# Where a two-layer diffusion and expert kernel loads its branch registers, makes its first weight splits and stores its output

## The chip, the cores and the metric

The kernel runs on one core of a Trainium2 chip. The metric is the device time of one execution in microseconds. Three runs of the kernel before gave 1623.38, 1624.77 and 1629.05 us; their median, 1624.77 us, is the time to compare with.

## The reference, cut to what matters

Two layers run over 256 latent tokens (and 256 context tokens) of width 1024. The change touches only the end of the second layer, a mixture of eight experts:

```python
logits = xt @ router_w + router_b            # 256 tokens, 8 experts
top_val, top_idx = lax.top_k(logits, 2)      # each token goes to its two best experts
gates = jax.nn.softmax(top_val)
# for each expert e, on the tokens that chose it:
y_e = (silu(x_e @ w1[e]) * (x_e @ w3[e])) @ w2[e]     # w1, w3: 1024x3584, w2: 3584x1024
out[token] += gate * y_e[token]
# behind it
xl = xl + g2 * out
return rms_norm(xl, final_g)
```

Everything is float32. An expert has 42 MB of weights and all eight are read once, 336 MB in all.

## The kernel before

**Places.** The experts are worked on one after the other in an order chosen at run time by how many tokens each has; the position in that order is called a place (0 to 7). Each place is cut into seven slices of 512 hidden columns. A slice is three steps on TensorE: `up` (the products with w1 and w3), `flip` (four or two transposes that turn the gated result so that it can be a stationary operand) and `lower` (the product with w2). `body(g)` runs `up` of slice g, then `lower` of slice g-1, then `flip` of slice g.

**Two ways to multiply.** Places 0, 1, 3, 5 and 7 are "raw" (`NAT` and `TWO`): at most 64 tokens, the float32 weights go straight into TensorE (`up_nat` with L1398, `flip_nat` with L1417 and the copy L1419, `down_nat` with L1428). Places 2, 4 and 6 hold up to 128 tokens and are "split" places: ScalarE casts each weight chunk of 128x1024 to a rounded high part (L163), VectorE subtracts it from the raw chunk to get the low part (L164), and TensorE makes three fast products with the parts (`mm3`, L266 to L268). The parts live in a ring of four chunks, `W_O` in the tiles R3 to R6. While a raw place runs, these tiles are lent out as extra landing room for weights (`lend`) and then taken back (`take_back`).

**Order of the work.** From the experts on, the program is written in manual order: what is called first stands first in each engine's queue, and each engine works through its queue in order. `w_split(n)` writes casts and subtractions until n chunks are split; `w_next` calls it so that the splits stay three chunks ahead of the products. An `agenda` of small steps (gathers of the next place, scatters of the last one) is run down between the products. `w_dma` puts the next 1 MB weight tile on SyncE's queue as soon as the written order has released a slot.

**Branches.** Places 0 and 7 exist in two versions, for up to 64 and for up to 128 tokens. `either` loads the count into a register of every engine (`values_load`, L1608), and a `tc.If(n > 64)` (L1610) picks the version. Behind place 7 a third branch, `tc.If(rv > 0)` (L1684, its register from L1683), runs an overflow pass for experts with more tokens than their place holds; with these inputs it is jumped over. The final norm (`inv_rms`, L735 and L256 to L262), the scaling (L1716, L1717) and the two stores (L1719) stand behind it.

**The end of place 7.** `scat_now` takes the expert's sum out of PSUM: weighted by the gate (first L1437), cast to a high part, the low part subtracted, eight products with the one-hot matrix (L1445, L1446), four additions to the tokens (L1450). `ends` then squares and sums each half row on ScalarE (L1643) and multiplies it by the final gain on GpSimd (L1644).

Of the kernel before, what the change touches and what calls it, by code (L numbers as in the profile page):

```python
# [8 lines left out]
F32 = mybir.dt.float32  # L9
# [6 lines left out]
P = 128  # L16
# [18 lines left out]
def tile_hybrid_headgroup_dit_moe(ctx: ExitStack, tc: tile.TileContext, a, out: bass.AP):  # L35
# [1383 lines left out]
            nc.scalar.copy(hs[n], b[:, 0:256])  # L1419
        return hs  # L1420

    def down_nat(p, i, hs, yas):
        for r in range(2):
            j, raw = raw_tile(("moe_w2", p, i))
            for jj in range(2):
                for hid_, ya in zip(hs, yas):
                    for hf in range(2):
                        nc.tensor.matmul(ya[64 * hf:64 * hf + 64, :], hid_[:, jj * P + 64 * r:jj * P + 64 * r + 64],  # L1428
                                         raw[:, 2 * hf + jj], start=i == 0 and r == 0 and jj == 0,
                                         stop=i == NSL - 1 and r == 1 and jj == 1, skip_group_check=True)  # L1430
                step()
            release(j)

    def scatter_nat(ya, v, g):
# [16 lines left out]
                r += [product, add]  # L1451
        return r

    def up(e, i, h, nxt):
        b1, b3 = bank(), bank()
        for w, b in (("moe_w1", b1), ("moe_w3", b3)):
            for c in range(4):
                wh, wl = nxt((w, e, i))
                for kk in range(2):
                    k = 2 * c + kk  # L1460
                    mm3(b, h.h[:, k], h.l[:, k], wh[:, kk * 512:kk * 512 + 512], wl[:, kk * 512:kk * 512 + 512],
                        k == 0, k == 7)
            if w == "moe_w1":
                s = sbuf[i % 2]
                nc.scalar.activation(s, b1, AF.Silu)
        nc.vector.tensor_mul(s, s, b3)
        return s
# [8 lines left out]
        nc.vector.tensor_sub(hl, b, hh)  # L1476
        return hh, hl

    def down(e, i, hth, ya, nxt):
        hh, hl = hth  # L1480
        for c in range(4):
            wh, wl = nxt(("moe_w2", e, i))
            for jj in range(2):
                j = c // 2 * 2 + jj
                mm3(ya[c % 2], hh[:, j * P:j * P + P], hl[:, j * P:j * P + P], wh[:, jj * 512:jj * 512 + 512],
                    wl[:, jj * 512:jj * 512 + 512], i == 0 and j == 0, i == NSL - 1 and j == 3)
# [54 lines left out]
    SCAT_N = [2, 6, 6, 14, 15, 18, 19, 34, 35, 38, 39]  # L1541
    ya = {}

    def lower(g, nat, two=False):
        e1, i1 = divmod(g, NSL)
        if i1 == 0:
            ya[e1] = [bank("acc") for _ in range(1 + two if nat else 2)]
        if nat:
            down_nat(e1, i1, hts.pop(g), ya[e1])
        else:  # L1550
            down(e1, i1, hts.pop(g), ya[e1], moe_next)
        if i1 == 4:
            gc = list(place(e1))[1]
            sl[:] = [slots(e1, one_hot(e1), gc)] + ([slots(e1, oh_2, gc, 1)] if two else [])
        if i1 == NSL - 1 and 0 < e1 < NE - 2:
            scat(e1, nat)
# [4 lines left out]
    def body(g, nat, two=False):  # L1561
        e, i = divmod(g, NSL)
        s = up_nat(e, i, two) if nat else up(e, i, hg[e], moe_next)
        if g and g - 1 in hts:
            lower(g - 1, nat if i else e - 1 in RAW, two)
            if i == 0 and 1 < e < NE - 1 and nat:
                lend(3, 4, 5, 6)
        hts[g] = flip_nat(g, s, two) if nat else flip(g, s)

    sl = []  # L1570

# [11 lines left out]
    def scat_now(p, more=None):  # L1583
        at = [0, 1, 2, 3, 4, 3, 5, 3, 6, 3, 7]
        for n, (y, (v, g)) in enumerate(zip(ya[p], sl)):
            plan_late(scatter_nat(y, v, g), [8 * n + x for x in at])
        if more is not None:
            plan_late(more, [8 * len(sl) + x for x in (-4, -3, -2, -1)])
        for fs in agenda:
            run(fs)  # L1590
        del agenda[:]
# [12 lines left out]
        scat_now(0)  # L1604


    def either(count, way):
        n = nc.values_load(count[0:1, 0:1], min_val=0, max_val=256)  # L1608
        saved, ends_at = state(), []
        with tc.If(n > 64) as cmp:  # L1610
            way(True)
# [7 lines left out]
            assert len(u) == len(v) and all(c is d or c == d or isinstance(c, tuple) and c[0] == d[0] and c[1] is d[1]  # L1619
                                            for c, d in zip(u, v)), x  # L1620

    either(first_n, first_place)
    take_back(0)
    regs.clear()
    LIM[0] = None
    for g in range(NSL, (NE - 1) * NSL):
        e, i = divmod(g, NSL)
        if i == 0:
            plan_late(fetch(e + 1, e + 1 in RAW), GATH)
        body(g, e in NAT)  # L1630
        if e in NAT and i == NSL - 1:
            take_back(3, 4, 5, 6)
            w_split(st["use"] + NW)
    lower((NE - 1) * NSL - 1, False)
# [10 lines left out]
    def last_place(two):  # L1645
# [4 lines left out]
            body((NE - 1) * NSL + i, True, two)  # L1650
        lower(LAST, True, two)
        nc.gpsimd.dma_start(fg, a["final_g"].to_broadcast([P, D]))
        scat_now(NE - 1, [lambda t=t, hf=hf: ends(t, hf) for hf in range(2) for t in range(2)])

    either(last_n, last_place)
    take_back(3, 4, 5, 6)


# [21 lines left out]
        return nxt  # L1680

    rest_r = [0]
    rv = nc.values_load(cmax[0:1, 0:1], min_val=0, max_val=256)  # L1683
    with tc.If(rv > 0):  # L1684
        for p in range(NE):
            nc.vector.tensor_scalar(posp[:, :, p], posp[:, :, p], 64.0 if p in NAT else 128.0, None, op0=OP.subtract)
# [23 lines left out]
        for t in range(2):  # L1710
            for hf in range(2):
                ends(t, hf)


    r = inv_rms(ss)
    nc.scalar.activation(xg[:, 0], xg[:, 0], AF.Copy, scale=r[:, 0:1])  # L1716
    nc.vector.tensor_scalar(xg[:, 1], xg[:, 1], r[:, 1:2], None, op0=OP.mult)  # L1717
    for t in range(2):
        (nc.scalar, nc.sync)[t].dma_start(out[t * P:t * P + P], xg[:, t])  # L1719


# [75 lines left out]
```

## Time and profile before

| | |
|---|---|
| three runs | 1623.38, 1624.77, 1629.05 us; median 1624.77 |
| the profiled execution | 1627.35 us, of which the span from the first to the last instruction is 1625.6 us |
| TensorE busy | 1561.9 us (96%) |
| VectorE, ScalarE, GpSimd busy | 933.0, 724.9, 25.9 us |
| mean granted TensorE clock | 0.978 |
| read from memory | 489.36 MB, 302 GB/s over the span |

The profiled execution has its own time, and a sum made from its rows is made against that. The trace can be asked for the order of time (what each engine did from when to when, and what ended the idle time before it), for the waits of an engine added up by what ended them, for all instructions of a line of the kernel, and for the busy time in any stretch. The busy share of TensorE says little by itself, since matmuls are pipelined and their ends are modelled; what it waited for is the better question.

### The profile page before, as it was taken

What the parts mean: (1) busy time and instruction counts of PE and PEld (TensorE: products, weight loads), DVE (VectorE), ACT (ScalarE), POOL (GpSimd) and SP (SyncE); (2) the same over time, 40 slices, a digit from 0 to 9 for tenths busy, and PEclk for the clock granted to TensorE, in tenths of its full rate; (3) what the DMA queues carried; (4) which work ended last, traced back from release to release, by engine and by line L of the source; (5) the groups of instructions that cost most, each with busy time, mean ns of one, the idle gap of its engine ahead of it and who ended that gap; (6) DMA issues with size and microseconds to landing.
All of it is one profiled execution on the core that took longest, in us unless ns stands there. A gap on an engine that the chain in (4) does not pass through costs nothing. (4 is left out here: it accounts for less than half of the span.)

```text
span 1625.6 us, 23224 instructions
## 1 busy us (share of the span) xinstructions
PE 1561.9 (96%) x8938; PEld 1161.5 (71%) x8938; DVE 933.0 (57%) x1587; ACT 724.9 (45%) x1085; POOL 25.9 (2%) x54
## 2 busy tenths in 40 slices
PE   7999999999999999999998999999999999999895
PEld 5787788888888887887654557875577855678652
DVE  3794578976564699856201038871188821688411
ACT  4446556222223474565311137761277711677301
POOL 0100000000000001000000000000000000000001
PEclk9999899999999999999799999999999999999998
DMA  8635323756674545547799999999999999999993
GB/s 349 241 137 187 121 83 130 273 200 234 218 276 167 184 165 185 199 181 266 303 421 421 421 421 420 422 403 422 420 421 421 384 420 421 421 421 385 396 420 130
DMA packets 69230, 492.09 MB, mean 303 GB/s; under 512 B 7984, under 2 KB 8752, under 8 KB 9712
## 3 DMA queue, kind: packets, MB, share of 16 engines
q1 hardware_dynamic: 67856, 486.97, 75.3%
q0 software_dynamic: 816, 2.72, 0.6%
q8 instruction: 76, 1.25, 0.3%
q10 hardware_dynamic: 432, 0.74, 0.2%
q14 instruction: 50, 0.41, 0.1%
HBM read 489.36 MB, written 1.05 MB: 302 GB/s over the span
## 5 line engine op out<-in xcount | busy, mean ns | idle before, releaser
L164 DVE TENSOR_TENSOR R<-FA,R 128x1024 fp32r<-128x1024 f32 x366 | 441.7, 1229 | 132.2 <-ACT R L163 128.1
L163 ACT CAST R<-FA 128x1024 fp32r<-128x1024 f32 x366 | 380.2, 1053 | 226.6 <-PE mm L268 142.4
L266 PE MATMUL mm<-R,R 128*128 128x512 f32 (+1 forms) x976 | 369.0, 379 | 9.8 <-ACT R L163 4.4
L267 PE MATMUL mm<-R,R 128*128 128x512 f32 (+1 forms) x976 | 364.1, 373 | 4.2 <-DVE R L164 2.3
L268 PE MATMUL mm<-R,R 128*128 128x512 f32 (+1 forms) x976 | 363.2, 372 | 0.0
L266 PEld LDWEIGHTS mm<-R,R 128*128 128x128 f32 x976 | 184.8, 190 | 48.4 <-ACT R L163 5.1
L266 PE MATMUL acc<-R,R 128*128 128x512 f32 (+1 forms) x552 | 208.2, 378 | 4.9 <-DVE R L788 1.8
L267 PEld LDWEIGHTS mm<-R,R 128*128 128x128 f32 x976 | 185.4, 190 | 36.2 <-DVE R L164 3.2
L268 PEld LDWEIGHTS mm<-R,R 128*128 128x128 f32 x976 | 185.3, 190 | 32.0
L268 PE MATMUL acc<-R,R 128*128 128x512 f32 (+1 forms) x552 | 204.6, 371 | 0.0
L267 PE MATMUL acc<-R,R 128*128 128x512 f32 (+1 forms) x552 | 204.5, 370 | 0.0
L1398 PE MATMUL mm<-FA 128*64 128x256 f32 x1408 | 163.8, 385 | 0.8 <-DVE FA L1450 0.8
L1398 PEld LDWEIGHTS mm<-FA 128*64 128x64 f32 x1408 | 98.8, 138 | 53.8 <-issue 7.4
L266 PEld LDWEIGHTS acc<-R,R 128*128 128x128 f32 x552 | 104.8, 190 | 26.4 <-issue 3.4
L268 PEld LDWEIGHTS acc<-R,R 128*128 128x128 f32 x552 | 104.4, 189 | 17.9 <-issue 0.3
L267 PEld LDWEIGHTS acc<-R,R 128*128 128x128 f32 x552 | 104.7, 190 | 16.5 <-issue 0.3
L1409 DVE TENSOR_TENSOR FA<-FA,mm 128x256 f32<-128x256 f32 x35 | 14.7, 421 | 152.6 <-PE mm L1398 152.6
L1428 PE MATMUL acc<-FA 128*64 128x512 f32 x424 | 99.0, 596 | 1.0 <-ACT FA L1419 1.0
L333 DVE SCALAR_TENSOR_TENSOR FA<-FA 128x1024 f32<-128x1024 f32 x80 | 94.4, 1222 | 5.7 <-DMA FA<-in_w_modt_dram 5.6
L499 DVE SCALAR_TENSOR_TENSOR FA<-FA,pv 128x512 f32<-128x512 f32 (+1 forms) x128 | 74.3, 616 | 1.2 <-ACT FA L495 0.7
L1343 DVE TENSOR_TENSOR R<-lc,R 128x128 fp32r<-128x128 f32 x24 | 7.0, 293 | 118.0 <-ACT R L1340 118.0
L1419 ACT COPY FA<-mm 128x256 f32<-128x256 f32 x35 | 13.1, 373 | 132.3 <-PE mm L1417 132.3
(275 smaller groups left out, 1397.8 us busy)
## 6 DMA issues: line engine op xcount, KB each, us to landing
FA<-in_moe_w_dram SPq DMA_DIRECT2D x264, 1024.0 KB, 15.3
R<-in_moe_w_dram SPq DMA_DIRECT2D x72, 1024.0 KB, 14.4
FA<-in_w_modt_dram SPq DMA_DIRECT2D x28, 1024.0 KB, 4.8
FA<-in_ffn_dram SPq DMA_DIRECT2D x22, 1024.0 KB, 4.8
FA<-in_ffn_w_dram SPq DMA_DIRECT2D x22, 1024.0 KB, 4.8
FA<-in_w_mod_dram SPq DMA_DIRECT2D x20, 1024.0 KB, 6.4
FA<-in_w_in_dram SPq DMA_DIRECT2D x20, 1024.0 KB, 4.8
FA<-in_w_out_dram SPq DMA_DIRECT2D x12, 1024.0 KB, 4.8
```

Source lines behind the costliest of these rows:

```text
L163: nc.scalar.copy(wh, raw)
L164: nc.vector.tensor_sub(wl, raw, wh)
L266: nc.tensor.matmul(ps, ll, rh, start=start, stop=False, skip_group_check=True)
L267: nc.tensor.matmul(ps, lh, rl, start=False, stop=False, skip_group_check=True)
L268: nc.tensor.matmul(ps, lh, rh, start=False, stop=stop, skip_group_check=True)
L333: nc.vector.scalar_tensor_tensor(o, raw[:, c], 1.0, csb[:, s], op0=OP.mult, op1=OP.mult, accum_out=modT[l][:, 2 * r + c, s:s + 1])
L499: nc.vector.scalar_tensor_tensor(acc, src, w, acc, op0=OP.mult, op1=OP.add)
L1343: nc.vector.tensor_sub(h.l[:, k], v["h32"], h.h[:, k])
L1398: nc.tensor.matmul(b[64 * c:64 * c + 64, 256 * n:256 * n + 256], hn[:, k], raw[:, q, 256 * c:256 * c + 256], start=k + n == 0, stop=k == 7 ...
L1409: nc.vector.tensor_mul(ss[n], ss[n], b[:, 256 * n:256 * n + 256])
L1419: nc.scalar.copy(hs[n], b[:, 0:256])
L1428: nc.tensor.matmul(ya[64 * hf:64 * hf + 64, :], hid_[:, jj * P + 64 * r:jj * P + 64 * r + 64], raw[:, 2 * hf + jj], start=i == 0 and r == ...
```

## The change

Five things move. The registers of the last two branches are loaded behind the first branch (`ln`, `rv`). Ahead of a split place the first four splits are written one slice earlier, behind the sixth slice of the raw place instead of behind its seventh. In the last slice of places 0, 6 and 7 the `flip` is written into the middle of `lower` of the slice before, so that ScalarE's copy of it runs beside the second half. The last place gets a scatter of its own, `scatter_last`: one weighting into SBUF, four float32 products, four additions, with the token half as the outer loop. And the final norm, scaling and stores become `finish()`, written ahead of the overflow branch, with the rows in two halves of 512 columns; the overflow pass calls it again at its end.

```diff
-    def down_nat(p, i, hs, yas):
+    def down_nat(p, i, hs, yas, mid=None):
         for r in range(2):
+            if r and mid:
+                mid()
             j, raw = raw_tile(("moe_w2", p, i))
...
+    def scatter_last(ya, v, g):
+        y = sbuf[0]
+        w = {}
+
+        def product(t, hf):
+            hp = slice(64 * hf, 64 * hf + 64)
+            w[t, hf] = bank()
+            nc.tensor.matmul(w[t, hf], v[hp, t * P:t * P + P].bitcast(F32), y[hp], start=True, stop=True)
+
+        def add(t, hf):
+            x = xs[:, 2 + t, 512 * hf:512 * hf + 512]
+            nc.vector.tensor_add(x, x, w[t, hf])
+        each = [(t, hf) for t in range(2) for hf in range(2)]
+        return [lambda: nc.vector.scalar_tensor_tensor(y, ya, g, gn, op0=OP.mult, op1=OP.mult)] \
+            + [lambda c=c: product(*c) for c in each] + [lambda c=c: add(*c) for c in each]
...
-    def down(e, i, hth, ya, nxt):
+    def down(e, i, hth, ya, nxt, mid=None):
         hh, hl = hth
         for c in range(4):
+            if c == 2 and mid:
+                mid()
...
     def body(g, nat, two=False):
         e, i = divmod(g, NSL)
         s = up_nat(e, i, two) if nat else up(e, i, hg[e], moe_next)
+        def turned():
+            hts[g] = flip_nat(g, s, two) if nat else flip(g, s)
+
+        early = i == NSL - 1 and e in (0, NE - 2, NE - 1) and not two
         if g and g - 1 in hts:
-            lower(g - 1, nat if i else e - 1 in RAW, two)
+            lower(g - 1, nat if i else e - 1 in RAW, two, turned if early else None)
             if i == 0 and 1 < e < NE - 1 and nat:
                 lend(3, 4, 5, 6)
-        hts[g] = flip_nat(g, s, two) if nat else flip(g, s)
+        if not early:
+            turned()
...
-    either(first_n, first_place)
+    either(nc.values_load(first_n[0:1, 0:1], min_val=0, max_val=256), first_place)
     take_back(0)
+
+    ln = nc.values_load(last_n[0:1, 0:1], min_val=0, max_val=256)
+    rv = nc.values_load(cmax[0:1, 0:1], min_val=0, max_val=256)
...
         body(g, e in NAT)
-        if e in NAT and i == NSL - 1:
+        if e in NAT and i == NSL - 2:
             take_back(3, 4, 5, 6)
             w_split(st["use"] + NW)
...
-    either(last_n, last_place)
+        scat_now(NE - 1, [lambda t=t, hf=hf: ends(t, hf) for t in range(2) for hf in range(2)])
+
+    either(ln, last_place)
+
+
+    def finish():
+        r = inv_rms(ss)
+        for hf in range(2):
+            c = slice(hf * 512, hf * 512 + 512)
+            nc.scalar.activation(xg[:, 0, c], xg[:, 0, c], AF.Copy, scale=r[:, 0:1])
+            nc.vector.tensor_scalar(xg[:, 1, c], xg[:, 1, c], r[:, 1:2], None, op0=OP.mult)
+            for t in range(2):
+                (nc.scalar, nc.sync)[t].dma_start(out[t * P:t * P + P, c], xg[:, t, c])
+    finish()
     take_back(3, 4, 5, 6)
...
-    r = inv_rms(ss)
-    nc.scalar.activation(xg[:, 0], xg[:, 0], AF.Copy, scale=r[:, 0:1])
-    nc.vector.tensor_scalar(xg[:, 1], xg[:, 1], r[:, 1:2], None, op0=OP.mult)
-    for t in range(2):
-        (nc.scalar, nc.sync)[t].dma_start(out[t * P:t * P + P], xg[:, t])
+        finish()
```

Three places of the written order, before and now. First ScalarE's queue around the last slice of place 1, ahead of the split place 2. L1407 is the silu of a raw slice, L1419 the copy of a flip, L163 the cast of a split; the R tiles of L163 are the ring of four. Before:

```order
L1354 CAST R_63<-mm 128x256
L1419 COPY FA<-mm 128x256
L1407 ACTIVATE FA<-mm 128x256
L1419 COPY FA<-mm 128x256
L163 CAST R_7762<-FA 128x1024
L163 CAST R_7763<-FA 128x1024
L163 CAST R_7764<-FA 128x1024
L163 CAST R_7765<-FA 128x1024
```

Now:

```order
L1354 CAST R_63<-mm 128x256
L1419 COPY FA<-mm 128x256
L163 CAST R_7736<-FA 128x1024
L163 CAST R_7737<-FA 128x1024
L163 CAST R_7738<-FA 128x1024
L163 CAST R_7739<-FA 128x1024
L1407 ACTIVATE FA<-mm 128x256
L1419 COPY FA<-mm 128x256
```

The four casts have moved in front of the silu and the flip copy of the last slice; the four subtractions on VectorE have moved in the same way, in front of that slice's gating multiplication.

Second TensorE's queue in the last slice of place 6. The four R tiles 10440 to 10443 (now 10414 to 10417) are the ring; L1472 (now L1491) is the flip. Before:

```order
L266 MATMUL acc<-R_10443,R_7319 128x512
L267 MATMUL acc<-R_10443,R_7319 128x512
L268 MATMUL acc<-R_10443,R_7319 128x512
L1472 MATMUL mm<-ident,lc 128x128 x4
L266 MATMUL acc<-R_10440,R_7319 128x512
L267 MATMUL acc<-R_10440,R_7319 128x512
```

Now:

```order
L266 MATMUL acc<-R_10415,R_7319 128x512
L267 MATMUL acc<-R_10415,R_7319 128x512
L268 MATMUL acc<-R_10415,R_7319 128x512
L1491 MATMUL mm<-ident,lc 128x128 x4
L266 MATMUL acc<-R_10416,R_7319 128x512
L267 MATMUL acc<-R_10416,R_7319 128x512
```

Before, the flip stands behind the fourth of the four chunks of `lower`, and the next product needs its result; now it stands behind the second, and two chunks follow that don't need it.

Third ScalarE's queue at the end. L1437 is the cast of the last sum, L1643 (now L1674) the squares of `ends`, L1684 (now L1725) the overflow branch. Before:

```order
L1419 COPY FA<-mm 128x256
L1437 CAST R_63<-acc 128x512
L1643 ACTIVATE FA,small<-FA 128x512 x4
L1610 UNCONDITIONAL_BRANCH
L1683 TENSOR_LOAD cmax
L1684 COMPARE_AND_BRANCH
```

Now:

```order
L1419 COPY FA<-mm 128x256
L1674 ACTIVATE FA,small<-FA 128x512 x4
L1638 UNCONDITIONAL_BRANCH
L1693 ACTIVATE FA<-FA,small 128x512
L1696 DMA out_dram<-FA 128x512
L1693 ACTIVATE FA<-FA,small 128x512
L1696 DMA out_dram<-FA 128x512
L1725 COMPARE_AND_BRANCH
```

The cast and the register load are gone from here, and scaling and stores stand ahead of the branch.

## Rows read from the trace of the kernel before

**Rows 1.** Busy time by stretch: start:end, length, us (instructions); clock, transfer share, GB/s.

```profile
1000.00:1100.00 100.00, 100.00 (x494) 80.08 (x492) 80.50 (x79) 68.24 (x78) 0.00 (x0) 1.00 1.00 414
```

**Rows 2.** Waits of TensorE, 780 to 1626 us: waiter <- releaser: total us, times, longest.

```profile
PE mm L266 <- ACT R L163: 4.4, 3, 1.5
PE mm L1398 <- issue: 4.1, 2, 2.4
PE mm L267 <- DVE R L164: 2.3, 3, 0.8
...
PE acc L266 <- DVE R L1476: 1.4, 1, 1.4
PE acc L1428 <- ACT FA L1419: 1.0, 2, 0.5
PE mm L1398 <- DVE FA L1450: 0.8, 1, 0.8
```

**Rows 3.** Order of time at places 1 and 2: start, us, engine, line, count [idle before].

```profile
952.64 0.39 ACT L1407 ACTIVATE FA<-mm 128x256 f32<-128x256 f32 x1 [3.24 <-PE mm L1398]
...
956.17 0.42 DVE L1409 TENSOR_TENSOR FA<-FA,mm 128x256 f32<-128x256 f32 x1 [6.85 <-PE mm L1398]
...
959.41 0.44 PE L1417 MATMUL mm<-ident,FA 128*128 128x128 f32 x2
959.94 0.37 ACT L1419 COPY FA<-mm 128x256 f32<-128x256 f32 x1 [6.91 <-PE mm L1417]
960.21 4.88 ACT L163 CAST R<-FA 128x1024 fp32r<-128x1024 f32 x5
961.29 4.63 DVE L164 TENSOR_TENSOR R<-FA,R 128x1024 fp32r<-128x1024 f32 x4 [4.70 <-ACT R L163]
```

**Rows 4.** SyncE's issues from 928 to 941 us, in order of time.

```profile
927.92 12.78 SPq L108 DMA_DIRECT2D FA<-in_moe_w_dram  x7
```

**Rows 5.** Weight transfers: engine, count, size, median us from issue to landing.

```profile
FA<-in_moe_w_dram SPq DMA_DIRECT2D x264, 1024.0 KB, 15.3
```

**Rows 6.** TensorE's loads and jumps at both versions: ns min/median/max, first and last start.

```profile
L1610 PEldq COMPARE_BRANCH  x2: 3777/4898/6019, 782.8 to 1519.9; - x2
...
L1608 PEldq TENSOR_LOAD <-ti x2: 308/399/490, 782.2 to 1519.5; - x2
```

**Rows 7.** Order of time at the end, place 7 and behind it.

```profile
1603.71 3.65 PE L1428 MATMUL acc<-FA 128*64 128x512 f32 x16 [0.52 <-ACT FA L1419]
...
1607.41 0.76 DVE L1437 SCALAR_TENSOR_TENSOR acc<-acc,gsb,FA 128x512 f32<-128x512 f32 x1 [7.48 <-PE acc L1428]
...
1609.66 0.80 PE L1445 MATMUL mm<-R 64*128 64x512 f32 x2 [2.30 <-DVE R L1437]
...
1611.72 4.94 POOL L1644 TENSOR_TENSOR FA<-FA 128x512 f32<-128x512 f32 x4 [9.44 <-DVE FA L1450]
1611.74 1.88 DVE L1450 TENSOR_TENSOR FA<-FA,mm 128x512 f32<-128x512 f32 x3 [0.17 <-PE mm L1446]
...
1613.71 0.61 ACT L1643 ACTIVATE FA<-FA 128x512 f32<-128x512 f32 x1
...
1617.35 0.16 DVE L735 SCALAR_TENSOR_TENSOR small<-small 128x2 f32<-128x2 f32 x1 [3.73 <-ACTq L1684]
...
1619.77 1.15 ACT L1716 ACTIVATE FA<-FA,small 128x1024 f32<-128x1024 f32 x1 [5.36 <-DVE small L262]
...
1620.95 0.36 ACTq L1719 DMA_DIRECT2D out_dram<-FA  x1
```

**Rows 8.** SyncE at the overflow branch (L1684): ns min/median/max, first and last start.

```profile
L1684 SPq EVENT_SEMAPHORE  x9: 17/17/17, 1586.8 to 1596.9; - x9
...
L1684 SPq COMPARE_BRANCH  x1: 45/45/45, 1581.5 to 1581.5; - x1
```

**Rows 9.** Busy time by stretch, behind place 0 and at the end; the clock is third from last.

```profile
870.00:880.00 10.00, 6.98 (x36) 3.17 (x34) 4.32 (x8) 0.59 (x1) 0.00 (x0) 0.78 1.02 424
1610.00:1620.00 10.00, 1.75 (x8) 0.90 (x6) 4.77 (x18) 2.90 (x9) 4.94 (x4) 0.50 0.02 7
```

More of the change, by code (lines that the diff above doesn't have):

```diff
@@ L1542, in tile_hybrid_headgroup_dit_moe, with lower @@
     ya = {}
-    def lower(g, nat, two=False):
+    def lower(g, nat, two=False, mid=None):
         e1, i1 = divmod(g, NSL)
@@ L1548, in lower @@
         if nat:
-            down_nat(e1, i1, hts.pop(g), ya[e1])
+            down_nat(e1, i1, hts.pop(g), ya[e1], mid)
         else:
-            down(e1, i1, hts.pop(g), ya[e1], moe_next)
+            down(e1, i1, hts.pop(g), ya[e1], moe_next, mid)
         if i1 == 4:
@@ L1585, in scat_now @@
         for n, (y, (v, g)) in enumerate(zip(ya[p], sl)):
-            plan_late(scatter_nat(y, v, g), [8 * n + x for x in at])
+            if p:
+                plan_late(scatter_last(y, v, g), [8 * n + x for x in (0, 1, 1, 2, 2, 3, 4, 5, 6)])
+            else:
+                plan_late(scatter_nat(y, v, g), [8 * n + x for x in at])
         if more is not None:
-            plan_late(more, [8 * len(sl) + x for x in (-4, -3, -2, -1)])
+            plan_late(more, [8 * len(sl) + x for x in (-5, -4, -3, -2)])
         for fs in agenda:
@@ L1604, in first_place, with either @@
         scat_now(0)
-    def either(count, way):
-        n = nc.values_load(count[0:1, 0:1], min_val=0, max_val=256)
+    def either(n, way):
         saved, ends_at = state(), []
@@ L1652, in last_place @@
         nc.gpsimd.dma_start(fg, a["final_g"].to_broadcast([P, D]))
-        scat_now(NE - 1, [lambda t=t, hf=hf: ends(t, hf) for hf in range(2) for t in range(2)])
-    either(last_n, last_place)
+        scat_now(NE - 1, [lambda t=t, hf=hf: ends(t, hf) for t in range(2) for hf in range(2)])
[9 more added lines that the diff above has]
+    finish()
     take_back(3, 4, 5, 6)
@@ L1682, in tile_hybrid_headgroup_dit_moe @@
     rest_r = [0]
-    rv = nc.values_load(cmax[0:1, 0:1], min_val=0, max_val=256)
     with tc.If(rv > 0):
```

## The prediction, made before the changed kernel ran

> **What bounds the kernel now.** I read the busy time by stretch first. In a stretch of a split place TensorE is busy for all of it and the transfers run at share 1.00 with 414 GB/s [rows 1], so either could be the bound. The waits decide it: from 780 us to the end TensorE waited for ScalarE, VectorE, jumps ("issue"), never for a transfer [rows 2]. So from the first expert on TensorE's own queue sets the time, and what counts is each place where it stands, and the chain behind its last product. The reader should see in [rows 2] that nearly all of this waiting sits at the points that the change touches: three starts of a split place (L266 and L267), the flip ahead of the last place (L1476), the two last raw flips (L1428 on L1419), the two jumps (L1398 on issue). Then I read the order of time at these points [rows 3, 7].
>
> The sum is made against the profiled execution: 1627.35 us, a span of 1625.6 and 1.75 around it. It ran 2.6 us above the median of the runs shown, 1624.77; I take the sum off the median.
>
> **Splits a slice earlier.** At the start of place 2 ScalarE's casts begin at 960.21, behind the copy of place 1's last flip, and VectorE's subtractions at 961.29 [rows 3]; TensorE, done with the flip at 959.85, waits for both. Over the three split places that is 4.4 and 2.3 us [rows 2], 2.2 a place, 6.7 together. Moved, four casts (4.88 for five, so 1.0 each) and four subtractions (4.63 in all) stand in front of the last slice's silu and gating multiplication. What hides them is idle time: ScalarE is idle 3.24 us before that silu at 952.64, that is from 949.4, and VectorE 6.85 before the multiplication at 956.17 [rows 3]. Have the tiles landed by then? The first two tiles of place 2 are the fourth and fifth of the seven issues from 927.92 [rows 4], at about 934 and 936; with the median of 15.3 us [rows 5] they land at about 949.4 and 951.5. So the casts run from 949.5 to about 953.7, the silu goes from 952.64 to 953.7, the subtractions end near 955.2, 1.0 us before the multiplication needs VectorE. That in turn has until the flip at 959.41, 2.8 us after its old end. Without that cover (tiles 3.8 us later) TensorE would pay each further us. What is late next at place 2 is the fifth chunk, whose ring slot comes free with the first chunk's products; a cast and a subtraction take 2.2 us, and the four chunks ahead are 24 products, at 494 matmuls in 100 us [rows 1] at least 4.9, so nothing. SyncE gets slots behind these splits in another order and may stand some us in front of one; up to 15.3 us of transfers are on their way [rows 5], so nothing. Bounds: 0 (the wait only moves) to 7.7 (what the first product itself loses by starting alone). I take 6.7.
>
> **Flips inside `lower`.** At places 0 and 7 TensorE waited 1.0 us for the copy [rows 2]; now half of `lower`, half of the 3.65 us of [rows 7], lies beside it. Gain 1.0, bounds 0 and 1.5. At place 6 the wait is 1.4 [rows 2], but behind it comes the jump to the last place.
>
> **The jump ahead of place 7.** TensorE's queue reached the load at 1519.5 and the jump at 1519.9, and the jump took 6.0 us [rows 6]; the engine itself stood for part of the 4.1 us of two jumps [rows 2]. Either the jump counts from when the queue reaches it, then finishing 1.4 earlier only makes TensorE stand longer and the gain is the load, 0.3 to 0.5 [rows 6]; or it counts from the last product, then the gain is 1.4 and the load. SyncE's jump took 5.3 us with no product ahead of it (1581.5 to 1586.8) [rows 8], which is nearer to the first. I take 0.7, bounds 0.3 and 1.9.
>
> [...] No run here shows what a jump is made of.
>
> **Loads behind place 0.** Two loads on each engine, 0.3 to 0.5 us each [rows 6]. On TensorE they stand where it waits 0.8 us for VectorE's additions [rows 2], its queue running ahead. I take 0; uncovered they cost 0.8. SyncE's two loads delay an issue by about a us, with 15 us of transfers on their way.
>
> **The end.** Before [rows 7]: sum weighted 1607.41 to 1608.17; cast and subtraction, and products from 1609.66; last three additions to 1613.62; ScalarE's last square to 1614.32; then VectorE waits until 1617.35, 3.73 us, for ScalarE, which is in the overflow jump. Now: products from 1608.3 (a handover costs 0.1, as from a cast's end at 961.19 to its subtraction at 961.29 [rows 3]). They are four in float32 of 512 columns in two pairs; `down_nat` gives the price, 16 records for eight such products in 3.65, so 0.9 a pair (if row halves run side by side as its column halves do; if not, 1.8 us more in all). First pair done at 1609.2, two additions (0.6 each, 0.2 behind) to 1610.7, the other two to 1612.0, last square 0.7 later as before, 0.2 to hand over, norm from 1612.9 instead of 1617.35: 4.45 earlier. The chain to the first scaling stays 2.42 (1617.35 to 1619.77). GpSimd, four multiplications in 4.94, ends at about 1615, as the scaling starts at 1615.3: no wait, though this is late next.
>
> [...]
>
> From the first scaling to the end of the span it was 5.8 us. Now ScalarE has two half scalings of 0.6 and two issues of 0.36, so the second store is out 1.9 behind the first scaling; from there to the end it was 4.3 (1621.3 to 1625.6), and a jump of about 3 (ScalarE, 1614.32 to 1617.35) lies beside the landing. Behind both come SyncE's nine semaphore steps of the skipped block, between 17 ns [rows 8] and a handover's 0.1 each; I take 0.6. So 6.8, a us more. Net gain 3.5; bounds 0 (a jump of 5.3 on SyncE as in [rows 8], products one by one) and 5.
>
> **Sum.** 6.7 + 1.0 + 0.7 + 0 + 3.5 = 11.9. 1624.77 - 11.9 = 1612.9, so 1613; against the profiled execution 1615.4.
>
> **Rivals.**
> Head start eaten up: VectorE, busy 80.5 of 100 us in a split place [rows 1] and with scatters on top early in it, falls behind and TensorE's wait comes back some chunks later. For it: its 1.2 us a chunk [rows 3] is what six products take at least by [rows 1]. Against: the waits list shows no later one at these places. The 6.7 is lost: 1619.6.
> [...]
> The upper bounds together (7.7, 1.5, 1.9, 5): 16.1, so 1608.7.
> The change doesn't do what it says at place 2, its tiles landing late: 2.2 less, 1615.
> Slower: supply becomes the bound. SyncE, standing in order in front of slots that the splits free, lets the transfers run dry at each of the three places. It decides from where the dry time exceeds the slack of the last weights (about 8.7 us, an estimate: the last tile, issued ahead of 1581.5 [rows 8], lands 15.3 later, and the second half of the last `lower` starts at 1605.5 [rows 7]) and the gain of 11.9: 20.6, or 6.9 a place. At 10 a place it is 1634. Against it: 15.3 us on their way at each place.
>
> **Chances.** The forecast with its own range of 1608.5 to 1617: 0.60; head start eaten up 0.12; clock better 0.06, clock worse 0.08; all upper bounds 0.05; place 2 late 0.05; supply 0.04. A change under 0.3%, 4.9 us, can't be told from none here, so faster means under 1619.9. Faster: all but supply, half of the eaten head start and a little for the spread of the runs (5.7 us among three), 0.87; same 0.09; slower 0.04. The range of 1606 to 1620 holds the bounds and half of the eaten head start.
>
> **What would show it.** Right: no wait of L266 and L267 at the three starts, the casts ahead of the silu, the norm starting under 6 us behind the last `down_nat` product. Wrong: a wait of TensorE for VectorE inside place 2, 4 or 6; a wait of TensorE for a transfer anywhere; a stand of well over 3 us at the jump ahead of place 7; the stores landing and then 3 us more until the end.

## The result, and the profile after

The changed kernel took 1613.3 us (median of five runs, 1611.4 to 1614.9) against 1624.8; the ratio is 0.9925, with a 95% interval of 0.9914 to 0.9936. The forecast was 1613 us, 11.9 faster; the runs say 11.5 faster. The sum behind it is less good than the total: two of its terms are wrong by 1.8 and 2.8 us, in opposite directions.

TensorE's waits from 780 us on, after (the columns as in [rows 2]):

```profile
PE mm L1417 <- DVE FA L1409: 2.8, 4, 1.2
PE mm L1447 <- DVE R L1439: 2.2, 1, 2.2
PE mm L1398 <- issue: 1.5, 1, 1.5
PE mm L1398 <- ACT lc L1323: 1.4, 1, 1.4
PE mm L1398 <- DVE FA L1452: 0.9, 1, 0.9
PE mm L1464 <- DVE lc L1470: 0.9, 1, 0.9
```

The waits of L266 and L267 at the three starts of a split place are gone, and so is that of the first `down` product of place 6. At the jump ahead of place 7 TensorE stands 1.5 us ("issue") instead of 2.4; its stand ahead of place 0, the other "issue" of [rows 2], is put down to ScalarE here (L1323). A wait for VectorE at a flip (L1417 on L1409) has grown, 1.2 us the longest. It is at the start of place 2, in order of time, after:

```profile
950.35 1.99 ACT L163 CAST R<-FA 128x1024 fp32r<-128x1024 f32 x2 [3.99 <-DMA FA<-in_moe_w_dram]
951.43 2.36 DVE L164 TENSOR_TENSOR R<-FA,R 128x1024 fp32r<-128x1024 f32 x2 [5.16 <-ACT R L163]
953.77 1.99 ACT L163 CAST R<-FA 128x1024 fp32r<-128x1024 f32 x2 [1.43 <-DMA FA<-in_moe_w_dram]
954.85 2.36 DVE L164 TENSOR_TENSOR R<-FA,R 128x1024 fp32r<-128x1024 f32 x2 [1.06 <-ACT R L163]
955.67 0.38 ACT L1407 ACTIVATE FA<-mm 128x256 f32<-128x256 f32 x1
957.13 0.41 DVE L1409 TENSOR_TENSOR FA<-FA,mm 128x256 f32<-128x256 f32 x1
957.60 0.44 PE L1417 MATMUL mm<-ident,FA 128*128 128x128 f32 x2 [1.15 <-DVE FA L1409]
957.79 0.48 PE L266 MATMUL mm<-R,R 128*128 128x512 f32 x1
958.11 0.39 PE L267 MATMUL mm<-R,R 128*128 128x512 f32 x1
```

The casts now stand ahead of the silu (L1407), as forecast, but they wait twice for their weights, 3.99 and 1.43 us. So the multiplication L1409 runs late and the flip with it. Before, TensorE waited here 1.5 for the first cast and 0.8 for the first subtraction instead [rows 2].

The end, in order of time, after, which answers to [rows 7]:

```profile
1588.78 5.37 PE L1430 MATMUL acc<-FA 128*64 128x512 f32 x24
1594.23 0.75 DVE L1470 SCALAR_TENSOR_TENSOR lc<-acc,gsb,FA 128x512 f32<-128x512 f32 x1 [6.92 <-PE acc L1430]
1595.03 1.99 PE L1464 MATMUL mm<-lc,R 64*128 64x512 f32 x8 [0.88 <-DVE lc L1470]
1596.19 2.48 DVE L1468 TENSOR_TENSOR FA<-FA,mm 128x512 f32<-128x512 f32 x4 [1.21 <-PE mm L1464]
1597.12 4.93 POOL L1675 TENSOR_TENSOR FA<-FA 128x512 f32<-128x512 f32 x4 [13.46 <-DVE FA L1468]
1599.51 0.16 DVE L735 SCALAR_TENSOR_TENSOR small<-small 128x2 f32<-128x2 f32 x1 [0.84 <-ACT FA L1674]
1599.71 1.15 DVE L256 TENSOR_SCALAR ti<-small 128x2 int32<-128x2 int32 x1
1600.77 0.16 DVE L257 TENSOR_SCALAR small<-small 128x2 f32<-128x2 f32 x1
1600.89 1.19 DVE L258 TENSOR_SCALAR small<-ti 128x2 int32<-128x2 int32 x1
1602.11 0.16 DVE L260 TENSOR_TENSOR small<-small 128x2 f32<-128x2 f32 x1
1603.92 0.72 ACT L1693 ACTIVATE FA<-FA,small 128x512 f32<-128x512 f32 x1 [4.44 <-issue]
```

The norm starts (L735) 5.4 us behind the last `down_nat` product instead of 10.0, as forecast. But L256 and L258, two operations on two elements a partition, take over a us each, and both end with a multiplication of GpSimd (L1675): L258 at 1602.08, the last of the four multiplications at 1602.05. The first scaling (L1693) comes 9.8 behind the last product, where the sum had about 8.0, and the span ends 7.5 behind it, where the sum had 6.8.

### The profile page after: what moved, and what is told of

It reads as the page before. It is cut to its first block, busy times and chain, and to the rows that moved or that the text cites. A ratio compares the mean times of both kernels' runs of the same rounds, so it can differ in the third digit from the quotient of the medians.

```text
span 1611.4 us, 23226 instructions
## 1 busy us (share of the span) xinstructions
PE 1557.2 (97%) x8938; PEld 1159.2 (72%) x8938; DVE 935.5 (58%) x1587; ACT 723.2 (45%) x1085; POOL 26.1 (2%) x54
## 5 line engine op out<-in xcount | busy, mean ns | idle before, releaser
L163 ACT CAST R<-FA 128x1024 fp32r<-128x1024 f32 x366 | 380.4, 1051 | 238.4 <-PE mm L268 139.3
L266 PE MATMUL mm<-R,R 128*128 128x512 f32 (+1 forms) x976 | 369.0, 379 | 5.4 <-DVE R L164 2.5
L267 PE MATMUL mm<-R,R 128*128 128x512 f32 (+1 forms) x976 | 363.9, 373 | 1.7 <-DVE R L929 1.6
L266 PEld LDWEIGHTS mm<-R,R 128*128 128x128 f32 x976 | 185.2, 190 | 43.1 <-ACT R L923 4.7
L266 PE MATMUL acc<-R,R 128*128 128x512 f32 (+1 forms) x552 | 208.3, 378 | 3.5 <-DVE R L788 1.8
L267 PEld LDWEIGHTS mm<-R,R 128*128 128x128 f32 x976 | 185.5, 190 | 32.8 <-DVE R L929 2.7
L267 PE MATMUL acc<-R,R 128*128 128x512 f32 (+1 forms) x552 | 204.5, 371 | 0.0
L266 PEld LDWEIGHTS acc<-R,R 128*128 128x128 f32 x552 | 104.7, 190 | 24.6 <-issue 3.4
L267 PEld LDWEIGHTS acc<-R,R 128*128 128x128 f32 x552 | 104.7, 190 | 16.6 <-issue 0.3
L1409 DVE TENSOR_TENSOR FA<-FA,mm 128x256 f32<-128x256 f32 x35 | 14.7, 421 | 131.5 <-PE mm L1398 131.5
L1419 ACT COPY FA<-mm 128x256 f32<-128x256 f32 x35 | 13.0, 372 | 119.7 <-PE mm L1417 119.7
```

Of the source, the lines that this page charges most:

```text
L163: nc.scalar.copy(wh, raw)
L266: nc.tensor.matmul(ps, ll, rh, start=start, stop=False, skip_group_check=True)
L267: nc.tensor.matmul(ps, lh, rl, start=False, stop=False, skip_group_check=True)
L1409: nc.vector.tensor_mul(ss[n], ss[n], b[:, 256 * n:256 * n + 256])
```

## The experiments

All kernels are measured by the stretch from one fixed point of TensorE's work to the next, since that repeats to some tenths of a us between profiles, while whole runs of a kernel spread over 1 to 9 us. The points are the first raw product of places 0 and 7, the first L267 of places 2, 4 and 6, the last `down_nat` product of place 7 and the span's end. "Median" is the time of the runs, with the ratio to the kernel before.

```
us                    0 to 2  2 to 4  4 to 6  6 to 7  place 7  end    median  ratio
before                175.8   214.9   214.9   133.7   81.3     18.2   1624.8
before, again         175.9   214.9   214.9   133.7   81.3     17.7   1624.2 (one run)
after                 172.9   212.2   212.2   131.0   80.7     17.3   1613.3  0.9925
after, again          172.7   212.1   212.2   131.4   80.7     17.3   1611.9  0.9925
splits late           173.9   216.5   215.0   131.2   80.8     17.4   1620.9  0.9975
flips late            172.6   212.1   212.2   131.1   81.3     17.3   1614.8  0.9929
norm late             172.3   212.2   212.2   130.9   80.7     15.7   1610.6  0.9905
gains apart           172.3   212.2   212.2   132.2   82.4     15.3   1612.3  0.9912
loads back            172.4   212.2   212.2   134.1   83.7     17.3   1618.1  0.9963
spare load            172.2   212.2   212.2   132.2   80.7     17.3   1613.6  0.9936
old scatter           173.4   212.2   212.2   131.1   80.7     18.3   1614.7  0.9931
norm late, gains      173.0   212.2   212.2   131.8   80.7     15.4   1611.1  0.9921
  and a square moved  172.8   212.2   212.2   130.9   80.7     16.0   1611.3  0.9919
  and place 0 fp32    173.2   214.3   212.2   131.0   80.7     15.5   1612.9  0.9923
```

**Splits late.**

```
-        if e in NAT and i == NSL - 2:
+        if e in NAT and i == NSL - 1:
```

> The changed kernel with the first splits of places 2, 4 and 6 back in the seventh slice of the place ahead. Theory: in the two traces the steps from place to place that hold such a start are 2.65 us shorter each after the change; of the one at place 2, 1.7 us belong to a shorter stretch at half clock behind place 0, which this edit leaves alone. So it loses 2.65 at places 4 and 6 and 1 to 2.65 at place 2: 6.3 to 8 us slower than the changed kernel (1613.3), some 1619.6 to 1621.3, and TensorE waits again for ScalarE and VectorE at L266 and L267, 2.2 us a place. Rival, the head start is paid back later in the place and the gain of those steps comes from the flips and the clock: under 3 us slower than the changed kernel, below 1616.3.

Measured 1620.9, 7.5 to 9 above the changed kernel; the waits of [rows 2] are back to the tenth:

```profile
PE mm L266 <- ACT R L163: 4.4, 3, 1.5
PE mm L267 <- DVE R L164: 2.3, 3, 0.8
```

The theory holds. The splits give 2.8 us each at places 4 and 6: the waits of 2.2, and about 0.4 more because the flip and the first products no longer follow one another closely (at place 4 the first L267 starts 3.2 us behind the flip here, as before, and 0.5 in the changed kernel). At place 2 the start comes 1.1 later, and 1.6 more are lost behind it to a stretch at half clock (962.9 to 966.3; half clock is a granted clock of 0.50, as from 876 to 882 before) that neither kernel before nor after has (1.00 from 962 to 967 in both), so by this run the splits there are worth 1.1 to 2.7; the two are not told apart.

**Flips late.**

```
-        early = i == NSL - 1 and e in (0, NE - 2, NE - 1) and not two
+        early = False
```

> The changed kernel with the last flips of places 0, 6 and 7 behind lower again. Theory: the flip at place 0 is worth 0.25 us by the step from place 0 to 1 and, since TensorE no longer stands there, 1.7 us more by the shorter stretch at half clock behind it; the flip at place 6 is worth 1.8 us in its own step, and with the shorter jump behind it 0.5 to 0.9 more; the one at place 7 is worth 0.6. Together 4.3 to 5.3 us slower than the changed kernel (1613.3), 1617.6 to 1618.6; the stretch at half clock behind place 0 is again about 7 us long instead of 3.4, and TensorE's jump ahead of place 7 about 6 us instead of 4.4. Rival, the length of the stretch at half clock changes from run to run by itself and the jump became shorter because the load ahead of it is gone: 1.0 us for places 0 and 7 and 1.4 for place 6 come back, 2.4 in all, 1615.7, with the stretch short and the jump at about 4.4.

Measured 1614.8, near the rival. From place 6 to 7 the flip itself costs what [rows 2] showed, but there is no "issue" wait at all: 131.1, as with the early flip. TensorE's waits from 1495 to 1530, flips late:

```profile
PE acc L266 <- DVE R L1495: 1.4, 1, 1.4
PE mm L1417 <- DVE FA L1409: 0.5, 1, 0.5
```

So TensorE reaches place 7 when its jump is over, whether it waits 1.4 us for the flip (131.1) or 1.5 for the jump (131.0, after). At place 7 the early flip gives 0.6. At place 0 it takes away the wait of 0.5, and place 1 starts 89.0 to 89.8 us behind place 0 with it (place 0 in fp32 aside) and 90.0 to 90.3 without (before, before again, flips late); by place 2 nothing of that shows (172.6). My guess that it shortens the stretch at half clock behind place 0 falls: that lasts 3.4 us here too, and in other kernels with the early flip (gains apart, loads back, square moved) 6.8, as before.

**Loads back.**

```
-    ln = nc.values_load(last_n[0:1, 0:1], ...)      # and rv, behind place 0
+    either(nc.values_load(last_n[0:1, 0:1], ...), last_place)   # rv behind it
```

> The changed kernel with the two register loads back at their branches, ahead of place 7 and ahead of the overflow branch. Theory: a load costs each engine its 0.3 to 0.5 us, and the jump behind it takes what it takes, 4.0 to 6.0, load or not: TensorE stands 0.3 to 0.5 longer ahead of place 7, and the end comes 0.4 later, since SyncE now has its load between the last store and the jump: 0.7 to 1 us slower than the changed kernel (1613.3), 1614.2. Rival: the load right ahead of it makes the jump longer (6.02 us in the kernel before, 3.96 to 5.54 in the four kernels without the load): the jump takes 6.0 again, and with the load 1.7 to 2.1 us are lost ahead of place 7, 1615.6 in all.

Measured 1618.1, 6.2 above the changed kernel in the same set; my theory was wrong by far, and the rival, right in kind, was too low. The jump took 7.0 us behind its load, and TensorE stood 4.5 for it. The jump and the waits of 1500 to 1530, loads back:

```profile
L1638 PEldq COMPARE_BRANCH  x1: 6979/6979/6979, 1507.3 to 1507.3; - x1
PE mm L1398 <- issue: 4.5, 1, 4.5
```

The same jump after, with the flips late, and with a spare load:

```profile
L1638 PEldq COMPARE_BRANCH  x1: 4359/4359/4359, 1508.9 to 1508.9; - x1
```
```profile
L1638 PEldq COMPARE_BRANCH  x1: 3959/3959/3959, 1510.4 to 1510.4; - x1
```
```profile
L1638 PEldq COMPARE_BRANCH  x1: 5399/5399/5399, 1508.2 to 1508.2; - x1
```

Behind the stand the granted clock fell to 0.66 on average, against 1.00 in the same window after, and place 7 took 3.0 us more. The window of 1512 to 1522 (clock last but two), loads back:

```profile
1512.00:1522.00 10.00, 7.54 (x43) 4.85 (x45) 0.00 (x0) 0.81 (x2) 0.00 (x0) 0.66 1.01 420
```

So the loads behind place 0 are worth 2.6 to 3.0 us ahead of place 7 (131.4 and 131.0 against 134.1) and, where the clock falls, 3.0 more. At the overflow branch the load costs nothing (17.3 both ways).

**Spare load.**

```
+    nc.values_load(last_n[0:1, 0:1], ...)      # unused
     either(ln, last_place)
```

> The changed kernel with a second, unused load of the same count on every engine right ahead of the branch to place 7; the branch itself goes by the register loaded behind place 0. With the load right ahead of the branch the jump took 6.02 us (before) and 6.98 (loads back), without it 3.96 to 5.54. Theory: what matters is that the branch's register has only just been loaded, so the spare load costs its own 0.3 to 0.5 us, the jump takes 4.0 to 5.5 again and the time is within 0.8 us of the changed kernel's (1613.3 and 1611.85 in two sets of runs). Rival: any load that stands ahead of the branch makes the jump longer: 6 to 7 us, TensorE stands 4 us or more there, the clock may fall behind it, and the time is 2.4 to 6 us longer, 1615 to 1618.

Measured 1613.6, as the theory had it, but "6 to 7" is 0.8 to 1.2 longer than in the changed kernel, and its jump of 5.4 lies in the upper part of the spread without a load, so it doesn't decide what in the load matters. **The kernel before and the changed kernel once more:**

> The kernel before once more, for a second profile of its jump ahead of place 7. Theory: with the load right ahead of it the jump takes 6 us or more, as in the first profile (6.02) and with the loads back (6.98), and TensorE stands over 2 us. Rival: the 6.02 was the upper end of the spread that the kernels without the load show (3.96 to 5.54), and this profile shows one of under 5.5.

> The changed kernel itself once more, as a measure of what one profile can tell. Theory: TensorE's jump ahead of place 7 and the stretches at half clock behind place 0 vary from one execution to the next (6.02 us before the change, 4.36 behind it, 3.96 with the flips late, 5.54 in the kernel that differs from the changed one only at its very end; 6.8 us at half clock before, 3.4 behind the change, 3.4 with late flips, 6.8 in the last of these). Then this profile shows some other pair of these values. Rival: both belong to the kernel's text, and this profile shows 4.36 us and 3.4 us again, to a tenth. The chain from the last down_nat product to the end of the span is 17.3 us in either case; median 1613.3, within 1.5.

The jump of the kernel before is 6.019 again:

```profile
L1610 PEldq COMPARE_BRANCH  x1: 6019/6019/6019, 1517.2 to 1517.2; - x1
```

With the branch's own load ahead of it the jump took 6.02, 6.02 and 6.98; without it 3.96 (flips late) to 5.54 (gains apart) in eight other kernels' profiles, and 4.36 and 4.76 in two of the changed one. That the load lengthens this jump is shown; how is not. At the overflow branch it doesn't: TensorE's jump there took 3.6 with it (before) and 3.3 (norm late) and 3.7 (after) without. And ahead of place 0, with its load right at it, the jump took 3.8 [rows 6], so a load at the branch doesn't by itself make a jump long.

**Norm late.**

```
-    finish()
     take_back(3, 4, 5, 6)
     ...
     with tc.If(rv > 0):
         ...
-        finish()
+    finish()
```

> The changed kernel with the last norm and the stores behind the overflow branch again; the last scatter in float32 and the early register loads stay. Theory: the norm ahead of the branch is worth little, because it runs beside GpSimd's multiplications and two of VectorE's operations in it, L256 and L258, take 1.15 and 1.19 us instead of 0.17. Behind the branch the norm starts some 3 us later, about 1602.5 instead of 1599.5 on the profile's clock, but all GpSimd work is over by then, so these operations take 0.17 again, and no jump follows the stores: 0 to 1.2 us slower than the changed kernel (1613.3), at most 1614.5. Rival, by the working of the prediction: 4.45 us from the earlier norm less 1.0 for the jump and the nine semaphore steps that now follow, 3.45 us slower, 1616.8.

Measured 1610.6, below both medians of the changed kernel (1613.3, 1611.9): the end takes 15.7 instead of 17.3. I had expected that it costs nothing to a little; that it gains 1.6 at the end was in neither theory. VectorE, norm late:

```profile
1595.12 2.48 DVE L1468 TENSOR_TENSOR FA<-FA,mm 128x512 f32<-128x512 f32 x4 [1.21 <-PE mm L1464]
1600.22 0.77 DVE L735 SCALAR_TENSOR_TENSOR small<-small 128x2 f32<-128x2 f32 x1 [2.62 <-ACTq L1724]
1601.03 0.17 DVE L256 TENSOR_SCALAR ti<-small 128x2 int32<-128x2 int32 x1
1603.25 0.72 ACT L1693 ACTIVATE FA<-FA,small 128x512 f32<-128x512 f32 x1 [4.85 <-DVE small L262]
```

The norm waits for ScalarE's jump again, yet its first scaling is only 0.4 later behind the last product, 10.2 against 9.8, since L256 and L258 are short, 0.17 us each. And behind it come 5.6 us, not 7.5, because no jump follows the stores. After, SyncE's queue reaches the overflow branch behind its second store and its semaphore steps 3.9 us later:

```profile
L1725 SPq EVENT_SEMAPHORE  x9: 17/17/17, 1609.2 to 1609.8; - x9
L1725 SPq COMPARE_BRANCH  x1: 45/45/45, 1605.3 to 1605.3; - x1
```

Then it has the closing steps of the whole program still to do, to 1610.6. That with the norm late these steps run beside the landing of the stores is my reading of the 5.6 us.

**Gains apart.** GpSimd multiplies only the first 128 rows, early; VectorE takes scale and gain of the others in one.

```
+        if t == 0:
             nc.gpsimd.tensor_tensor(xg[:, t, c], xs[:, 2 + t, c], fg[:, c], op=OP.mult)
-    nc.vector.tensor_scalar(xg[:, 1, c], xg[:, 1, c], r[:, 1:2], None, op0=OP.mult)
+    nc.vector.scalar_tensor_tensor(xg[:, 1, c], xs[:, 3, c], r[:, 1:2], fg[:, c], op0=OP.mult, op1=OP.mult)
```

> The changed kernel with GpSimd multiplying by the gain only for the first 128 rows (two multiplications of 1.26 us instead of four); for the second 128 rows VectorE multiplies by the scale and the gain in one operation. GpSimd is then done at about 1599.6 on the profile's clock, as the norm starts. Theory: VectorE's L256 and L258 each waited for GpSimd's operation to end; they take 0.17 us again, the first scaling starts 1.9 us earlier, and the kernel is 1.5 to 2 us faster than the changed one (1613.3): 1611.3 to 1611.8. Rival, these two operations on int32 are slow here for another reason (the ScalarE results just ahead of them, or their type after a long stretch without it): they still take 1.1 to 1.2 us and the time stays within 0.4 us of 1613.3, or gets 0.2 to 0.4 worse by the longer operation on VectorE.

The theory holds at the end, which takes 15.3 instead of 17.3; the median is 1.0 lower, where 1.5 to 2 were expected. In order of time:

```profile
1600.03 2.49 POOL L1676 TENSOR_TENSOR FA<-FA 128x512 f32<-128x512 f32 x2 [13.46 <-DVE FA L1468]
1602.42 0.16 DVE L735 SCALAR_TENSOR_TENSOR small<-small 128x2 f32<-128x2 f32 x1 [0.83 <-ACT FA L1674]
1602.62 0.17 DVE L256 TENSOR_SCALAR ti<-small 128x2 int32<-128x2 int32 x1
1602.82 0.17 DVE L258 TENSOR_SCALAR small<-ti 128x2 int32<-128x2 int32 x1
1604.83 0.72 ACT L1694 ACTIVATE FA<-FA,small 128x512 f32<-128x512 f32 x1 [2.44 <-issue]
```

The first scaling is now 7.8 behind the last product (1597.07), about what the prediction had (8.0). The profiled run itself, 1614.2, is the longest of the six; in it the jump ahead of place 7 took 5.54 us and the clock fell behind it (1515.7 to 1519.1; 0.89 granted on average from 1505 to 1520, against 1.00 after): 2.9 us in the columns "6 to 7" and "place 7".

The rows show what the long times go with. After, L256 and L258 take 1.15 and 1.19 us and each ends within 0.03 us of the end of one of GpSimd's multiplications; with no multiplication beside them, as here, they take 0.17. The additions L1468, which read one input from a bank of products (mm), take 0.7 us each, after, both ahead of the multiplications and beside them. Why the ones are held up and the others not, no run shows. The profile counts the standing as the operation's own time, so no list of waits shows it: VectorE's waits from 1590 to 1612, after, are 6.9 and 1.2 for TensorE and 0.8 for ScalarE, none for GpSimd.

**Norm late, gains apart.** Both edits.

> The last norm behind the overflow branch, as in the fastest kernel so far, and GpSimd multiplying by the gain only for the first 128 rows. In that kernel the norm's first operation on VectorE, L735, took 0.77 us instead of 0.16, ending with GpSimd's last multiplication but one. Theory: any operation of VectorE's norm may be held up by GpSimd, not only the two on int32; with GpSimd done early L735 takes 0.16, and from the last down_nat product to the end of the span it is 15.1 us instead of 15.7. Rival: L735 was waiting for ScalarE's semaphore step behind its jump and the profile shows that as its time: it still takes about 0.8 and the chain stays at 15.7 or gets 0.2 longer by the longer operations on VectorE. The median, 1610, can't tell the two apart.

L735 takes 0.16 us and the end 15.4, 0.3 better than with the norm late alone:

```profile
1601.92 0.16 DVE L735 SCALAR_TENSOR_TENSOR small<-small 128x2 f32<-128x2 f32 x1 [2.67 <-ACTq L1725]
```

So an operation of the norm that isn't on int32 can be held up too: with the norm late L735 took 0.77. (It ended there at 1600.99, with GpSimd's last multiplication, 1600.97, not the last but one.) It is also where the gain stops: with GpSimd out of the way, the norm ahead of the branch (15.3) and behind it (15.4) are worth the same. The earlier start is given back by the jump behind the stores.

**And a square moved** from ScalarE to VectorE:

```
+        if (t, hf) == (1, 1):
+            nc.vector.scalar_tensor_tensor(o, x, 1.0, x, op0=OP.mult, op1=OP.mult, accum_out=acc)
+        else:
+            nc.scalar.activation(o, x, AF.Square, accum_out=acc)
```

> The kernel with the norm behind the branch and GpSimd's share halved, and the last of the four squares done by VectorE instead of ScalarE. Theory: a jump counts from when the engine's queue reaches it, and ScalarE's was the last to end ahead of the norm (1597.64 to 1600.17, VectorE's 1596.03 to 1599.03); with one square less its queue reaches the jump 0.6 us earlier and VectorE's 0.6 later, so the norm starts 0.5 earlier: 14.6 us from the last down_nat product to the end of the span, against 15.1. Rival: a jump can't end before the engine's work ahead of it, and VectorE, which has the fourth square behind its fourth addition, is then the late one: its jump ends 0.7 later than before and the chain stays at 15.1 to 15.3.

The rival, and worse: 16.0. VectorE's queue reaches the branch only at 1598.93, with the start of its square, and its jump is the late one. The square takes 1.45 us, twice the 0.7 of other such operations (L1699), with GpSimd's multiplications beside it until 1599.81; that they hold it up too is likely, not shown. It runs beside the jump:

```profile
1597.32 2.49 POOL L1680 TENSOR_TENSOR FA<-FA 128x512 f32<-128x512 f32 x2 [13.46 <-DVE FA L1468]
1598.91 1.45 DVE L1676 SCALAR_TENSOR_TENSOR FA<-FA 128x512 f32<-128x512 f32 x1
1602.18 0.16 DVE L735 SCALAR_TENSOR_TENSOR small<-small 128x2 f32<-128x2 f32 x1 [1.81 <-DVEq L1729]
```

**And place 0 in fp32** (on "norm late, gains apart"):

```
-            if p:
+            if True:
                 plan_late(scatter_last(y, v, g), ...)
```

> The kernel with the norm behind the overflow branch and GpSimd's share halved, and the scatter of place 0 in float32 too, as that of place 7. Theory: TensorE's wait of 2.2 us for the cast and the subtraction ahead of place 0's products falls to 0.9, as at place 7, and four products pairs take about as long as the eight fast ones: place 1 starts 1.3 to 1.6 us earlier after place 0, and with less standing the stretch at half clock there may go, 1.7 to 3.4 more: 1608 to 1610 against 1611.1. Rival: the additions, 2.5 us for four, set the start of place 1 as before, TensorE waits for them instead, and the clock falls anyway: within 0.5 us of 1611.1.

Place 1 does start about 1.1 us earlier, and the half clock behind place 0 is gone (1.00 from 870 to 880). But the tiles of place 2 come no sooner:

```profile
951.49 1.99 ACT L163 CAST R<-FA 128x1024 fp32r<-128x1024 f32 x2 [7.70 <-DMA FA<-in_moe_w_dram]
957.69 0.69 PE L1417 MATMUL mm<-ident,FA 128*128 128x128 f32 x2 [3.82 <-DVE FA L1409]
```

TensorE waits 3.8 us for the flip instead of 1.4 ("norm late, gains apart"), and the clock falls at the start of place 2 (956.4 to 963.2; 0.66 granted on average from 955 to 965). So place 2 is at the limit of the transfers, which run at a share of 1.00 to 1.02 from 900 to 960 before and after and of 1.02 from 955 to 965 here, and time won ahead of it is lost there. The column "0 to 2" says the same: it is 172.2 to 173.4 in every kernel with the early splits, whether TensorE ran 0, 3.4 or 6.8 us at half clock behind place 0.

**Old scatter** at place 7, on the changed kernel, with the steps of `ends` in the order that went with it.

```
-            if p:
+            if False:
                 plan_late(scatter_last(y, v, g), ...)
```

> The changed kernel with the old last scatter (cast, subtraction and two fast products a piece) at place 7. Theory: the four float32 products take the place of a cast, a subtraction and eight products; by the two traces the last addition ends 4.5 us behind the last down_nat product with them and 6.3 without, so the chain from that product to the end of the span is 1.8 longer, 19.1 us instead of 17.3, and the time about 1615 by the first set of runs of the changed kernel, 1613.7 by the second. Rival: part of these 1.8 us is given back, since GpSimd's multiplications, which hold up the norm, come 1.2 us apart and start by the first additions: the chain is under 18.2.

The end takes 18.3, 1.0 more: the theory's 1.8 was too much, the rival is nearer. The two traces of before and after differ by 1.8 at the last addition, but in the one before the old products ran at half clock (0.50 from 1610 to 1614, 0.67 to 0.80 us a pair of records); here a pair took 0.43 to 0.51.

No experiment gives a version that beats the changed kernel beyond doubt. From the last product to the end of the span "norm late, gains apart" and "gains apart" are 1.9 and 2.0 us shorter, "norm late" 1.6; by the runs the ratio intervals to the kernel before (0.9907 to 0.9934, 0.9896 to 0.9928, 0.9890 to 0.9921) overlap that of the change.

## Why the prediction held, and where it did not

By the two profiles of each kernel the change gives 3.1 up to place 2, 2.8 and 2.8 in the next two stretches, 2.5 from place 6 to 7, 0.6 in place 7 and 0.7 at the end: 12.4 us. The terms, in the prediction's order:

- **Splits**, 6.7: right, and at places 4 and 6 a little low (2.8 against 2.2 each, above the upper bound of 7.7 for three). At place 2 the tiles came late, the rival that was given 0.05, but without the 2.2 lost: the wait moved to the flip and was 1.15, in place of two waits of 2.2 together. The working took 15.3 us, the median of all weight transfers, from issue to landing; in the trace of before the two tiles, issued at 933.9 and 935.6, took 18.3 and 19.8, so they landed at 952.2 and 955.4 and not at 949.4 and 951.5. The cover of 3.8 us that the working had found takes nearly all of that. TensorE waits because it now comes to the flip sooner, 171.2 us behind the start of place 0 instead of 172.6: in the three kernels with early splits that ran 6.8 us at half clock behind place 0, as before did (gains apart, loads back, square moved), it waits there 0, 0 and 0.3, and "0 to 2" is no longer than after.
- **Flips at places 0 and 7**, 1.0: 0.6 at place 7; what place 0 wins is gone at place 2.
- **Jump ahead of place 7**, 0.7: the first of my two readings, that the jump counts from when the queue reaches it, is borne out by the late flips (no stand at the jump, and 131.1 against 131.0 and 131.4). Its price for the load was wrong: not 0.3 to 0.5 but 2.3 to 2.6 in the sum, since the jump itself is shorter without the load right ahead of it (4.4 and 4.8 us in the two profiles after, 6.0 in both before). That is more than the upper bound of 1.9. The step that failed is "the gain is the load, 0.3 to 0.5".
- **Loads behind place 0**, 0: right; with the loads back place 1 starts 89.1 us behind place 0, within the 89.0 to 89.8 of the kernels that have them there.
- **End**, 3.5: failed; it is 0.4 to 0.9. The norm did start 4.6 us earlier behind the last product, but "the chain to the first scaling stays 2.42" is wrong, since it is 4.4 beside GpSimd's multiplications. I had looked at GpSimd only as the one that the scaling might wait for. And "a jump of about 3 ... lies beside the landing" fails on SyncE, whose jump of 3.9 has the program's closing steps behind it: 7.5 instead of 6.8. With the first cured, the norm ahead of the branch is worth no more than behind it.

The end's loss of 2.8 is made up by the jump (1.8 more), the splits of places 4 and 6 (1.1 more) and the stretch up to place 2 (0.8 more). The total was right by terms that cancel; that it came within a us was luck.

Of the rivals, the eaten head start, the dry transfers and the worse clock did not come (after, the granted clock was 1.00 from 1505 to 1530 and, at the last products, from 1590 to 1600); the clock behind place 0 was a little better in both profiles after (3.4 us at half clock instead of 6.8; 0.83 of full from 870 to 880 instead of 0.78, [rows 9]). That this comes of the change is not shown: three of the kernels with it had 6.8 too, and their "0 to 2" was no longer for it.

## What to carry to other kernels

Before work is moved beside other work, ask not only whether the engines are free but whether they hold each other up: here VectorE operations of 0.17 us on the path took 1.15 and 1.19 beside GpSimd's multiplications of 1.26. A register that a branch needs may be better loaded long ahead of it than at it; here that paid 2.6 to 3.0 us at one branch and made no difference at another (17.3 us both ways). Work moved ahead of a jump puts the jump behind it: here SyncE, which issues last, pays 3.9 us for it at the end.

## What the runs showed of the hardware

- The overflow branch, which is taken, has a record of 45 to 56 ns on the other engines (before, after, norm late), but their next step comes 2.5 us (ScalarE, norm late) to 5.3 us later (SyncE, before [rows 8]); ahead of place 7 SyncE's came after 0.4 (before, after). On TensorE the record itself is 3.3 us (norm late, at the overflow branch) to 7.0 (loads back, ahead of place 7). It runs beside work that is already queued: in the kernel with the norm late VectorE's queue was at the branch from 1596.03 to 1599.03, and two of its additions ran in that time. At the overflow branch, with the weights' transfers over (a share of 0.01 from 1590 to 1600, after), TensorE's took 3.3 to 3.7; ahead of place 7, in the midst of transfers (a share of 0.97 from 1505 to 1526 before, 0.99 from 1505 to 1520 after, 1.01 from 1512 to 1522 with the loads back), 4.0 to 7.0. No run here separates the transfers from other causes.
- The granted clock fell behind a stand of 4.5 us (loads back: 0.66 on average from 1512 to 1522) and one of 2.7 (gains apart: 0.89 from 1505 to 1520) at the jump ahead of place 7, but not behind another of 2.7 (spare load: 1.00 from 1512 to 1522) or of 2.4 (before: 1.00 from 1520 to 1530).
